# First norm centred and scaled 1024 columns at a time in place, and half of the key weights' subtractions moved to GpSimd

## The chip, the cores and the metric

The kernel runs on one core of one Trainium2 chip. The metric is device time in microseconds (us) of one execution; the median of three runs of the kernel before is 990.82 us. Engines are named as in the profile: PE (TensorE matmuls), PEld (its weight loads), DVE (VectorE), ACT (ScalarE), POOL (GpSimd), SP (the queue that issues most DMAs).

## What is computed

A trunk of two layers over 256 tokens of width 2048: first a Mamba-2 layer, then a layer of sliding-window attention. Each ends in a residual sum and a layer norm. The change lies where the first layer ends and the second begins:

```python
x = _layernorm(ALPHA * x + h, ln_g[0], ln_b[0])    # end of the Mamba-2 layer
...
kv = x @ kv_w + kv_b                               # shared keys and values: 2048 x 512
...
proj = x @ w_in                                    # queries and gates: 2048 x 4096

def _layernorm(x, g, b):
    mu = jnp.mean(xf, axis=-1, keepdims=True)
    var = jnp.mean(jnp.square(xf - mu), axis=-1, keepdims=True)
    return (xf - mu) * lax.rsqrt(var + EPS) * g + b
```

## The kernel before

**Products.** Every float32 product is made of three matmuls in the fp32r type: each operand is split into a high part (a rounded copy) and a low part (the operand minus its high part), and high x high, high x low and low x high are summed in PSUM.

**Weight units.** Weights come from HBM in units of 128 x 2048, each as two halves of 128 x 1024. SP loads a half into a raw buffer `wr` (five of them). ACT copies it into the high part `wh` (`load_unit`, L143), and DVE subtracts: `wl = wr - wh` (L144). `wh` and `wl` have four buffers each, so the copy of a new unit waits until PE has done with the unit four places earlier; a raw buffer is free for the next load when its subtraction has read it. The numbers behind the names count buffers: the four units of the keys' and values' weights (`wkv`) have `wl_881`, `wl_886`, and then `wl_916` and `wl_920` before, `wl_908` and `wl_912` in the changed kernel.

**The end of the first layer.** The 256 tokens are two row halves, h = 0 and h = 1, of 128 tokens; both lie in `xr`. `out_last` multiplies the last group of the Mamba layer with four units of the output weights. For each unit (512 columns, `nb`) PE makes 12 matmuls (L330 to L332), DVE adds the sum to `xr` (L337) and takes statistics (L809). All four column blocks of h = 0 come first, and then `done1(0)` runs; blocks 1 to 3 of h = 1 follow, and then `done1(1)`.

**`done1(h)`**, the first norm, takes mean and variance together (L813), makes the reciprocal deviation on ACT (L815, L816), and then goes through four blocks c of 512 columns: DVE centres and multiplies by the gain (L831, from `xr` into a buffer `t`), scales and adds the bias (L834, back to `xr`); PE transposes the block, four matmuls against the identity (L839, into PSUM); ACT copies the result into the high part `x1H` (L844), DVE makes the low part `x1L` (L845).

**Keys and values.** `x_stat` (L881 to L883) multiplies `x1H` and `x1L` with the four `wkv` units, for h = 0 and then for h = 1: 48 matmuls each. L881 needs `x1H` and `wh`, L882 `x1L`, L883 `wl`. Unit i uses the columns of block c = i of the norm; its first two of four steps read the first halves of `wh` and `wl`, the last two the second halves. Of the bias of keys and values POOL issues the load (L859), and the sums are added on DVE (L897, L901).

**The order.** In the Mamba layer the order on each engine is that of the code. In everything named above a scheduler sets it, engine by engine, by its own costs and priorities; each engine then works through its row strictly in that order.

Of the kernel before, what the change touches and what calls it, by code (L numbers as in the profile page):

```python
# [8 lines left out]
F32 = mybir.dt.float32  # L9
# [3 lines left out]
ALU = mybir.AluOpType  # L13
AX = mybir.AxisListType

P = 128
# [3 lines left out]
NG = 8  # L20
# [42 lines left out]
def trunk(ctx: ExitStack, tc: tile.TileContext, A: dict, out: bass.AP, dbg=None):  # L63
    nc = tc.nc
    PSUM = bass.MemoryType.PSUM

    def pool(name, bufs=1, side=None, space=None, stack=ctx):
        kw = {"space": space} if space is not None else {}
        return stack.enter_context(
            tc.tile_pool(name=name, bufs=bufs, side=side, reuse_waits="tile", **kw)  # L70
        )
# [9 lines left out]
    def nm(s):  # L81
        uid[0] += 1
        return f"{s}_{uid[0]}"
# [4 lines left out]
    def ax_tile():  # L88
        return ax_ps.tile([P, 512], F32, tag="ax", name=nm("ax"), bufs=4)
# [27 lines left out]
    def new_unit(places):  # L117
        u = Unit()
        u.parts = []
        for tag, n, pl in (("wh", NH, places[0]), ("wl", NL, places[1])):  # L120
            t = wp.tile([P, 2112], F32R, tag=tag, name=nm(tag), bufs=n)
            u.parts.append([(t[:, o : o + (k1 - k0) * P], k0, k1) for o, k0, k1 in pl])
        u.h, u.l = u.parts[0][0][0], u.parts[1][0][0]
        return u
# [3 lines left out]
    def load_half():  # L128
        if halves:
            n, c = halves.pop(0)  # L130
            raws[n, c] = raw = wp.tile([P, 1024], F32, tag="wr", name=nm("wr"), bufs=NR)
            nc.sync.dma_start(raw[:], srcs[n][:, c * 1024 : (c + 1) * 1024])

    def load_unit(n, places):
        u = new_unit(places)
        for c in range(2):
            half = raws.pop((n, c))
            for (h, k0, k1), (l, _, _) in zip(*u.parts):
                a, b = max(k0, 8 * c), min(k1, 8 * c + 8)
                if a < b:  # L140
                    sl = slice((a - k0) * P, (b - k0) * P)
                    raw = half[:, (a - 8 * c) * P : (b - 8 * c) * P]
                    nc.scalar.activation(h[:, sl], raw, AF.Copy)  # L143
                    nc.vector.tensor_tensor(l[:, sl], raw, h[:, sl].bitcast(F32), ALU.subtract)  # L144
            load_half()
        return u

# [72 lines left out]
    srcs = []  # L220

    def wo_srcs(name, j):
        return [A[name][j * 4 + i] for i in range(4)]

    for g in range(NG):
# [3 lines left out]
                srcs.append(A["wo"][(g - 1) * 4 + OUT_AT[g].index(b)])  # L229
        if g > 0:  # L230
            srcs += [A["wo"][(g - 1) * 4 + i] for i in range(len(OUT_AT[g]), 4)]
    srcs += wo_srcs("wo", NG - 1) + [A["wkv"][i] for i in range(4)]
    broken = set()
    for what, j in B_ORDER:
        if what == "g":
# [13 lines left out]
    def fill_units():  # L249
        while len(units) < min(used[0] + ahead[0], len(srcs)):  # L250
            n = len(units)
            if n == MORE_AT:
                ahead[0] = AHEAD
            if n in XK_AT:
                i = XK_AT.index(n)
                nc.sync.dma_start(xr[:, i, :], A["xk"][:, i, :])
            if n - 2 in XK_AT:
                i = XK_AT.index(n - 2)
                nc.scalar.activation(xr[:, i, :], xr[:, i, :], AF.Copy, scale=ALPHA)
            units.append(load_unit(n, BROKEN if n in broken else [WHOLE, WHOLE]))  # L260
# [35 lines left out]
    xr = xr_all[:, : 2 * D].rearrange("p (h d) -> p h d", h=2)  # L296
# [44 lines left out]
    def out_last(aH, aL, rms, stats, done):  # L341

        us = []
        for nb in range(4):
            us.append(next_unit())
            out_unit(aH, aL, 0, us[nb], nb, False, rms)
            stats(0, nb)
            if nb == 0:
                out_unit(aH, aL, 1, us[nb], nb, False, rms)
                stats(1, nb)  # L350
        done(0)
        for nb in range(1, 4):
            out_unit(aH, aL, 1, us[nb], nb, False, rms)
            stats(1, nb)
        done(1)
# [403 lines left out]
    for g in range(NG):  # L759
        t = 10 * g  # L760
# [47 lines left out]
    def norm_stats(st, h, nb):  # L808
        nc.vector.bn_stats(st[:, h, nb, :], xr[:, h, nb * 512 : (nb + 1) * 512])  # L809

    def norm_scale(lp, st, h):
        mv = lp.tile([P, 2], F32, tag="mv", name=nm("mv"), bufs=2)
        nc.vector.bn_aggr(mv[:], st[:, h, :, :])  # L813
        rs = lp.tile([P, 1], F32, tag="rs", name=nm("rs"), bufs=2)
        nc.scalar.activation(rs[:], mv[:, 1:2], AF.Ln, bias=eps_t[:])  # L815
        nc.scalar.activation(rs[:], rs[:], AF.Exp, scale=-0.5)  # L816
        return mv, rs

    with ExitStack() as s2:
        lp = pool("lp", stack=s2)  # L820
        gb = lp.tile([P, 2, D], F32, tag="gb", name="gb1")
        nc.gpsimd.dma_start(gb[:, 0, :], A["lng"][0].partition_broadcast(P))
        nc.gpsimd.dma_start(gb[:, 1, :], A["lnb"][0].partition_broadcast(P))
        st1 = lp.tile([P, 2, 4, 6], F32, tag="st", name="st1")

        def done1(h):
            mv, rs = norm_scale(lp, st1, h)
            for c in range(4):
                sl = slice(c * 512, (c + 1) * 512)
                t = lp.tile([P, 512], F32, tag="t", name=nm("t"), bufs=2)  # L830
                nc.vector.scalar_tensor_tensor(  # L831
                    t[:], xr[:, h, sl], mv[:, 0:1], gb[:, 0, sl], ALU.subtract, ALU.mult
                )
                nc.vector.scalar_tensor_tensor(  # L834
                    xr[:, h, sl], t[:], rs[:], gb[:, 1, sl], ALU.mult, ALU.add
                )
                ps = ax_tile()
                for k in range(4):
                    nc.tensor.transpose(  # L839
                        ps[:, k * P : (k + 1) * P], xr[:, h, c * 512 + k * P : c * 512 + (k + 1) * P], ident  # L840
                    )
                dst = (slice(None), slice(c * 4, c * 4 + 4), slice(h * P, (h + 1) * P))
                psv = ps[:].rearrange("p (k t) -> p k t", k=4)
                nc.scalar.activation(x1H[dst], psv, AF.Copy)  # L844
                nc.vector.tensor_tensor(x1L[dst], psv, x1H[dst].bitcast(F32), ALU.subtract)  # L845

        if PRE:
            tc.keep_in_program_order(nc.scalar.preload_act_table_set("natural_log_exp_and_others"))
        out_last(*gs[NG - 1].y, gs[NG - 1].rms, lambda h, nb: norm_stats(st1, h, nb), done1)
    a_stack.close()  # L850

# [393 lines left out]
```

## Time and profile before

| | |
|---|---|
| median of 3 runs (990.53 to 991.11) | 990.82 us |
| profiled execution, its time | 993.6 us |
| its span, first to last instruction | 991.8 us |
| its mean granted TensorE clock | 0.994 |
| PE busy | 980.7 us, 99% of the span |
| DVE busy | 795.7 us, 80% |
| ACT busy | 534.5 us, 54% |
| POOL busy | 170.1 us, 17% |

Times inside the kernel are counted from the span's start. The norm and the keys' and values' products take the stretch from about 650 to 690. "x2" behind a row says that two neighbouring instructions of one form are shown as one row, with the time from the start of the first to the end of the second. In square brackets stands the idle time ahead of an instruction, and what ended it. A row of the form "746/750/1794" gives the shortest, the median and the longest duration in ns. POOL's subtractions, of which the change makes four, have no row in this profile; POOL's other two-input operations have.

### The profile page before, as it was taken

The page shows a single profiled execution, that of the slowest core. Times are in us where ns is not written, and L with a number is a line of the kernel's source. Part 1 is how long each engine was busy: PE and PEld are TensorE (multiplying, and loading weights), DVE is VectorE, ACT ScalarE, POOL GpSimd, SP SyncE. Part 2 cuts the span into 40 slices and gives each one's busy share as a digit, 9 for nine tenths or more (in the row PEclk, how much of TensorE's full clock was granted, in tenths as well). Part 3 has the DMA queues.
Part 4 walks back from the last instruction along what each step waited for, and adds up shares of the span by engine and source line. Part 5 has one row for each costly group of instructions (what it writes and reads, how often), then busy time and mean ns, then how long its engine had stood idle before and what let it go on. Part 6 is the DMA issues. An engine that isn't in the chain of part 4 may idle for free.

```text
span 991.8 us, 17619 instructions
## 1 busy us (share of the span) xinstructions
PE 980.7 (99%) x6868; PEld 881.7 (89%) x6868; DVE 795.7 (80%) x1227; ACT 534.5 (54%) x905; POOL 170.1 (17%) x225
## 2 busy tenths in 40 slices
PE   9999999999999999999999999999999999999997
PEld 7999989999998998999999999877898888878875
DVE  6879887976987887796797697999658687878686
ACT  6586747455644835744745554444446454635432
POOL 0004004005046002200400400500202222221102
PEclk9999999999999999999999999999999999999998
DMA  9588885686585666658558657646774849584932
GB/s 367 178 281 271 253 290 153 187 298 174 172 306 178 209 197 242 203 183 308 151 186 304 170 171 261 241 147 218 226 234 140 313 153 327 166 305 119 340 115 86
DMA packets 69443, 218.72 MB, mean 221 GB/s; under 512 B 8096, under 2 KB 19632, under 8 KB 68592
## 3 DMA queue, kind: packets, MB, share of 16 engines
q1 hardware_dynamic: 63648, 198.95, 61.5%
q0 software_dynamic: 5424, 18.12, 5.4%
q8 instruction: 54, 0.88, 0.4%
q10 hardware_dynamic: 288, 0.52, 0.1%
q14 instruction: 29, 0.24, 0.1%
HBM read 205.37 MB, written 12.19 MB: 219 GB/s over the span
## 4 chain that ended last, share of the span: by engine, by line
PE 78%; DVE 11%; ACT 4%; DMA 4%; issue 3%; POOL 0%; DVEq 0%; SPq 0%; POOLq 0%; ACTq 0%
PE mm L269 14%; PE mm L270 14%; PE mm L271 14%; PE mm L330 7%; PE mm L331 7%; PE mm L332 7%; PE mm L881 3%; DVE wl L144 3%; PE mm L882 3%; PE mm L883 3%; PE ax L609 2%; ACT wh L143 1%; DMA pd<-z 1%; PE ax L1007 1%; DMA gb<-in_lng 1%
## 5 line engine op out<-in xcount | busy, mean ns | idle before, releaser
L144 DVE TENSOR_TENSOR wl<-wr,wh 128x1024 fp32r<-128x1024 f32 (+2 forms) x338 | 398.6, 1209 | 92.7 <-ACT wh L143 91.8
L143 ACT ACTIVATE wh<-wr 128x1024 fp32r<-128x1024 f32 (+2 forms) x338 | 328.9, 1012 | 197.1 <-PE mm L331 71.7
L269 PE MATMUL mm<-xH,wh 128*128 128x256 f32 x1280 | 356.2, 278 | 0.0
L270 PE MATMUL mm<-xL,wh 128*128 128x256 f32 x1280 | 355.2, 278 | 0.0
L271 PE MATMUL mm<-xH,wl 128*128 128x256 f32 x1280 | 354.9, 277 | 0.0
L269 PEld LDWEIGHTS mm<-xH,wh 128*128 128x128 f32 x1280 | 240.8, 188 | 3.5 <-issue 0.9
L270 PEld LDWEIGHTS mm<-xL,wh 128*128 128x128 f32 x1280 | 240.8, 188 | 1.0
L271 PEld LDWEIGHTS mm<-xH,wl 128*128 128x128 f32 x1280 | 240.7, 188 | 0.0
L626 POOL TENSOR_TENSOR yz<-yz,z 128x256 f32<-128x256 f32 x32 | 33.3, 1060 | 437.6 <-DVE yz L620 431.5
L330 PE MATMUL mm<-wh,yH 128*128 128x512 f32 x256 | 101.4, 396 | 1.9 <-DVE xr L337 1.9
L331 PE MATMUL mm<-wh,yL 128*128 128x512 f32 x256 | 100.0, 391 | 0.0
L332 PE MATMUL mm<-wl,yH 128*128 128x512 f32 x256 | 99.8, 390 | 0.0
L457 DVE SCALAR_TENSOR_TENSOR cv<-mm,pc,cv 128x255 f32<-128x255 f32 x144 | 69.2, 481 | 15.3 <-ACT cv L455 11.8
L270 PE MATMUL mm<-x1L,wh 128*128 128x256 f32 x256 | 70.9, 277 | 0.0
L269 PE MATMUL mm<-x1H,wh 128*128 128x256 f32 x256 | 70.8, 277 | 0.0
L271 PE MATMUL mm<-x1H,wl 128*128 128x256 f32 x256 | 70.8, 277 | 0.0
L881 PE MATMUL mm<-wh,x1H 128*128 128x512 f32 x160 | 63.8, 398 | 0.0
L883 PE MATMUL mm<-wl,x1H 128*128 128x512 f32 x160 | 62.8, 392 | 0.3 <-DVE wl L144 0.2
L882 PE MATMUL mm<-wh,x1L 128*128 128x512 f32 x160 | 62.7, 392 | 0.2 <-DVE x1L L845 0.2
L455 ACT ACTIVATE cv<-mm,pc 128x256 f32<-128x256 f32 x48 | 26.8, 558 | 63.6 <-PE mm L271 63.5
L330 PEld LDWEIGHTS mm<-wh,yH 128*128 128x128 f32 x256 | 48.1, 188 | 12.5 <-DVE xr L337 2.3
L332 PEld LDWEIGHTS mm<-wl,yH 128*128 128x128 f32 x256 | 48.1, 188 | 10.1
(222 smaller groups left out, 1378.7 us busy)
## 6 DMA issues: line engine op xcount, KB each, us to landing
wr<-in_wa SPq DMA_DIRECT2D x154, 512.0 KB, 5.3
wr<-in_wo SPq DMA_DIRECT2D x64, 512.0 KB, 5.1
wr<-in_wq SPq DMA_DIRECT2D x32, 512.0 KB, 5.1
wr<-in_wg SPq DMA_DIRECT2D x32, 512.0 KB, 5.4
wr<-in_wb SPq DMA_DIRECT2D x32, 512.0 KB, 5.3
rb<-rscr SPq DMA_DIRECT2D x16, 512.0 KB, 5.9
el<-rscr SPq DMA_DIRECT2D x16, 256.0 KB, 7.6
wr<-in_wkv SPq DMA_DIRECT2D x8, 512.0 KB, 6.6
```

Source lines behind the costliest of these rows:

```text
L143: nc.scalar.activation(h[:, sl], raw, AF.Copy)
L144: nc.vector.tensor_tensor(l[:, sl], raw, h[:, sl].bitcast(F32), ALU.subtract)
L269: nc.tensor.matmul(ps, ah, bh, start=first, stop=False)
L270: nc.tensor.matmul(ps, ah, bl, start=False, stop=False)
L271: nc.tensor.matmul(ps, al, bh, start=False, stop=last)
L330: nc.tensor.matmul(ps[:], aH[:, k, hs], u.h[:, ks], start=k == 0, stop=False)
L331: nc.tensor.matmul(ps[:], aL[:, k, hs], u.h[:, ks], start=False, stop=False)
L332: nc.tensor.matmul(ps[:], aH[:, k, hs], u.l[:, ks], start=False, stop=k == 3)
L457: nc.vector.scalar_tensor_tensor(a[:, sft:], ps[:, : S - sft], w(3 - sft), a[:, sft:], ALU.mult, ALU.add)
L881: nc.tensor.matmul(ps[:], x1H[:, kk, hs], u.h[:, ks], start=kk == 0, stop=False)
L882: nc.tensor.matmul(ps[:], x1L[:, kk, hs], u.h[:, ks], start=False, stop=False)
L883: nc.tensor.matmul(ps[:], x1H[:, kk, hs], u.l[:, ks], start=False, stop=kk == KT - 1)
```

## The change

In `done1` the two DVE operations are done on 1024 columns, at c = 0 and c = 2, and in place: the buffer `t` goes. So eight operations for each row half become four. Transposes and splits stay at 512 columns. In `load_unit` the subtraction of the second half (c = 1) of the four `wkv` units goes to GpSimd.

```diff
-                    nc.vector.tensor_tensor(l[:, sl], raw, h[:, sl].bitcast(F32), ALU.subtract)
+                    eng = nc.gpsimd if c and len_a <= n < len_a + 4 else nc.vector
+                    eng.tensor_tensor(l[:, sl], raw, h[:, sl].bitcast(F32), ALU.subtract)
...
-    srcs += wo_srcs("wo", NG - 1) + [A["wkv"][i] for i in range(4)]
+    srcs += wo_srcs("wo", NG - 1)
+    len_a = len(srcs)
+    srcs += [A["wkv"][i] for i in range(4)]
...
             for c in range(4):
-                sl = slice(c * 512, (c + 1) * 512)
-                t = lp.tile([P, 512], F32, tag="t", name=nm("t"), bufs=2)
-                nc.vector.scalar_tensor_tensor(
-                    t[:], xr[:, h, sl], mv[:, 0:1], gb[:, 0, sl], ALU.subtract, ALU.mult
-                )
-                nc.vector.scalar_tensor_tensor(
-                    xr[:, h, sl], t[:], rs[:], gb[:, 1, sl], ALU.mult, ALU.add
-                )
+                if c % 2 == 0:
+                    v = xr[:, h, c * 512 : (c + 2) * 512]
+                    g, b = [gb[:, i, c * 512 : (c + 2) * 512] for i in range(2)]
+                    nc.vector.scalar_tensor_tensor(v, v, mv[:, 0:1], g, ALU.subtract, ALU.mult)
+                    nc.vector.scalar_tensor_tensor(v, v, rs[:], b, ALU.mult, ALU.add)
```

The diff adds lines, so numbers shift: L144 becomes L145, L330 to L332 become L333 to L335, L337 becomes L340, L809 becomes L812, L813 becomes L816; the two operations of the norm, L831 and L834, become L835 and L836; L839 to L883 stay.

The scheduler also writes another order around the norm. DVE, from the mean and variance of h = 0 on, before:

```order
L813 BN_AGGR mv_890_7586<-st1_7479 128x2
L831 SCALAR_TENSOR_TENSOR t_892_7591<-xr_76,mv_890_7586,gb1_7476 128x512
L831 SCALAR_TENSOR_TENSOR t_894_7601<-xr_76,mv_890_7586,gb1_7476 128x512
L834 SCALAR_TENSOR_TENSOR xr_76<-t_892_7591,rs_891_7588,gb1_7476 128x512
L144 TENSOR_TENSOR wl_886_7562<-wr_868_7420,wh_885_7561 128x1024
L144 TENSOR_TENSOR wl_886_7562<-wr_877_7515,wh_885_7561 128x1024
L845 TENSOR_TENSOR x1L_7472<-ax_893_7594,x1H_7471 128x4x128
L834 SCALAR_TENSOR_TENSOR xr_76<-t_894_7601,rs_891_7588,gb1_7476 128x512
L831 SCALAR_TENSOR_TENSOR t_896_7611<-xr_76,mv_890_7586,gb1_7476 128x512
L831 SCALAR_TENSOR_TENSOR t_898_7621<-xr_76,mv_890_7586,gb1_7476 128x512
```

DVE at the same place in the changed kernel:

```order
L816 BN_AGGR mv_890_7586<-st1_7479 128x2
L835 SCALAR_TENSOR_TENSOR xr_76<-xr_76,mv_890_7586,gb1_7476 128x1024 x2
L145 TENSOR_TENSOR wl_886_7562<-wr_868_7420,wh_885_7561 128x1024
L836 SCALAR_TENSOR_TENSOR xr_76<-xr_76,rs_891_7588,gb1_7476 128x1024 x2
L340 SCALAR_TENSOR_TENSOR xr_76<-mm_896_7623,r_872_7453,xr_76 128x512
L845 TENSOR_TENSOR x1L_7472<-ax_892_7593,x1H_7471 128x4x128
L845 TENSOR_TENSOR x1L_7472<-ax_893_7600,x1H_7471 128x4x128
L845 TENSOR_TENSOR x1L_7472<-ax_894_7609,x1H_7471 128x4x128
L845 TENSOR_TENSOR x1L_7472<-ax_895_7616,x1H_7471 128x4x128
```

All 2048 columns are now centred first, then one weight half is subtracted, then all columns are scaled; before, the first 512 columns were scaled ahead of that weight unit.

PE, with the first transposes of h = 0, before (the block of `xr` that they turn goes to `ax_893`):

```order
L331 MATMUL mm_901_7646<-wh_865_7412,yL_864_7403 128x512
L332 MATMUL mm_901_7646<-wl_866_7413,yH_863_7402 128x512
L839 MATMUL ax_893_7594<-cc_69,xr_76 128x128 x4
L330 MATMUL mm_901_7646<-wh_865_7412,yH_863_7402 128x512
L331 MATMUL mm_901_7646<-wh_865_7412,yL_864_7403 128x512
```

PE with all transposes of h = 0 in the changed kernel; the first row here stands twelve matmuls behind the second row above:

```order
L335 MATMUL mm_898_7653<-wl_876_7512,yH_863_7402 128x512
L839 MATMUL ax_892_7593<-cc_69,xr_76 128x128 x4
L839 MATMUL ax_893_7600<-cc_69,xr_76 128x128 x4
L333 MATMUL mm_898_7653<-wh_875_7511,yH_863_7402 128x512
L839 MATMUL ax_894_7609<-cc_69,xr_76 128x128 x4
L839 MATMUL ax_895_7616<-cc_69,xr_76 128x128 x4
L334 MATMUL mm_898_7653<-wh_875_7511,yL_864_7403 128x512
L335 MATMUL mm_898_7653<-wl_876_7512,yH_863_7402 128x512
L333 MATMUL mm_898_7653<-wh_875_7511,yH_863_7402 128x512
L334 MATMUL mm_898_7653<-wh_875_7511,yL_864_7403 128x512
L335 MATMUL mm_898_7653<-wl_876_7512,yH_863_7402 128x512
L881 MATMUL mm_906_7716<-wh_880_7536,x1H_7471 128x512
```

The sixteen transposes now stand close together, ahead of the first matmul for the keys; before, the last eight stood between the first of those. For h = 1 they likewise move into one place.

POOL in the changed kernel, behind the loads of gain and bias (before, those were followed by the loads of `snk` and `bias` directly):

```order
L826 DMA gb1_7476<-in_lnb 128x2048
L145 TENSOR_TENSOR wl_881_7537<-wr_867_7416,wh_880_7536 128x1024
L145 TENSOR_TENSOR wl_886_7562<-wr_877_7515,wh_885_7561 128x1024
L145 TENSOR_TENSOR wl_908_7718<-wr_882_7540,wh_907_7717 128x1024
L145 TENSOR_TENSOR wl_912_7740<-wr_887_7565,wh_911_7739 128x1024
L855 DMA snk_7710<-in_snk 128x32
L859 DMA bias_905_7714<-in_kvb 128x512
```

The four subtractions now stand ahead of those two loads. On ACT the copies of the third `wkv` unit (`wh_907`) now stand ahead of the four copies into `x1H` of h = 0, and those of the fourth (`wh_911`) behind them. From the sums of h = 1 (L897 for the second time) on every engine has its old order again.

## The prediction

> **What bounds the kernel now.** I read the page's engine shares first, then PE's timeline through the stage of the norm, then DVE's and ACT's beside it, and last every place where POOL and DVE run side by side.
>
> ```profile
> PE 980.7 (99%) x6868; PEld 881.7 (89%) x6868; DVE 795.7 (80%) x1227; ACT 534.5 (54%) x905; POOL 170.1 (17%) x225
> ```
>
> PE is the bound nearly everywhere, so this stage can give only what PE loses in it. PE there:
>
> ```profile
> 656.06 0.39 PE L332 MATMUL mm<-wl,yH 128*128 128x512 f32 x1
> 656.44 0.63 PE L839 MATMUL ax<-cc,xr 128*128 128x128 f32 x4
> 656.82 0.48 PE L330 MATMUL mm<-wh,yH 128*128 128x512 f32 x1
> 657.14 0.40 PE L331 MATMUL mm<-wh,yL 128*128 128x512 f32 x1
> ...
> 664.14 0.40 PE L882 MATMUL mm<-wh,x1L 128*128 128x512 f32 x1
> ...
> 668.26 0.39 PE L882 MATMUL mm<-wh,x1L 128*128 128x512 f32 x1
> 668.83 0.50 PE L883 MATMUL mm<-wl,x1H 128*128 128x512 f32 x1 [0.17 <-DVE wl L144]
> ...
> 673.88 1.29 PE L839 MATMUL ax<-cc,xr 128*128 128x128 f32 x8 [0.29 <-DVE xr L834]
> 675.20 0.50 PE L881 MATMUL mm<-wh,x1H 128*128 128x512 f32 x1
> 675.93 0.50 PE L882 MATMUL mm<-wh,x1L 128*128 128x512 f32 x1 [0.22 <-DVE x1L L845]
> ...
> 681.00 0.48 PE L881 MATMUL mm<-wh,x1H 128*128 128x512 f32 x1
> ```
>
> Undisturbed matmuls follow each other every 0.229 us (664.14 to 668.26, 18 steps). Four transposes take 0.38 (656.44 to 656.82), and the step after them 0.32, 0.09 more than usual. From the L332 at 656.06 to the L881 at 681.00 PE's row holds 82 matmuls and eight groups of four transposes, in seven runs: 82 x 0.229 + 8 x 0.38 + 7 x 0.09 = 22.45 us. It took 24.94, so 2.5 us are lost, to `wl`, to the scaled `xr` and to `x1L`: all late from DVE. The same two instructions stand in the changed row with the same work between them, only that the groups form four runs (22.2 us). So the change is worth 22.2 - 24.94 = -2.75 us, plus what PE then waits.
>
> **Part one: 1024 columns, in place.** DVE and ACT in h = 0:
>
> ```profile
> 653.92 0.26 DVE L813 BATCH_NORM_AGGREGATE mv<-st 128x2 f32<-128x24 f32 x1
> 654.22 1.41 DVE L831 SCALAR_TENSOR_TENSOR t<-xr,mv,gb 128x512 f32<-128x512 f32 x2
> 655.55 0.74 DVE L834 SCALAR_TENSOR_TENSOR xr<-t,rs,gb 128x512 f32<-128x512 f32 x1
> 656.22 2.35 DVE L144 TENSOR_TENSOR wl<-wr,wh 128x1024 fp32r<-128x1024 f32 x2
> ...
> 664.52 1.28 DVE L845 TENSOR_TENSOR x1L<-ax,x1H 128x512 fp32r<-128x512 f32 x2
> 665.71 1.28 DVE L809 BATCH_NORM_STATS2 st<-xr 128x6 f32<-128x512 f32 x2
> 654.90 2.01 ACT L143 ACTIVATE wh<-wr 128x1024 fp32r<-128x1024 f32 x2 [0.15 <-PE mm L331]
> 658.27 2.01 ACT L143 ACTIVATE wh<-wr 128x1024 fp32r<-128x1024 f32 x2 [0.56 <-PE mm L331]
> ```
>
> A 512-wide operation of the norm occupies DVE for 0.66 us (655.55 - 654.22, halved), a 1024-wide subtraction for 1.13 (2.35 less one of 1.22, at 656.22). A 1024-wide operation of the norm has no row; it lies between 1.13 and 2 x 0.66 = 1.32, and I take 1.2. Four for each h in place of eight save 0.5 us of DVE per h. The price is lumpiness: no column is scaled before all are centred. Centring runs from 654.22 to 656.6, one weight half to 657.75, and undisturbed the scaled halves would be ready at 658.95 and 660.15. PE's twelve matmuls ahead of the transposes cover the first: 656.06 + 13 x 0.229 = 659.04. Covered, the lumps cost nothing; without that cover each tenth of a microsecond of lateness is one for PE.
>
> **Part two: four subtractions on POOL.** They take 4 x 1.13 = 4.5 us from DVE. POOL itself is idle here, and its results are early enough: the tightest, the fourth, is done about 671 by the times below and read by PE about 676. What it does to DVE is another matter:
>
> ```profile
> L1143 DVE SCALAR_TENSOR_TENSOR t<-xr,mv,gb x4: 746/750/1794, 974.8 to 976.8; 128x512 f32<-128x512 f32 x4
> L1147 POOL TENSOR_TENSOR xr<-t,gb x4: 1272/1426/1747, 976.5 to 980.9; 128x512 f32<-128x512 f32 x4
> L339 DVE TENSOR_TENSOR xr<-xr,mm x3: 669/674/689, 978.5 to 981.2; 128x512 f32<-128x512 f32 x3
> L144 DVE TENSOR_TENSOR wl<-wr,wh x338: 244/1220/1760, 21.2 to 961.5; 128x1024 fp32r<-128x1024 f32 x153, 128x128 fp32r<-128x128 f32 x8, 128x896 fp32r<-128x896 f32 x8
> L630 POOL TENSOR_TENSOR sq<-yz x32: 608/1191/1610, 90.4 to 632.5; 128x256 f32<-128x256 f32 x32
> 236.67 3.26 DVE L144 TENSOR_TENSOR wl<-wr,wh 128x1024 fp32r<-128x1024 f32 x2
> 237.24 1.60 POOL L630 TENSOR_TENSOR sq<-yz 128x256 f32<-128x256 f32 x1
> 238.92 1.60 POOL L634 TENSOR_TENSOR sq<-sq,sq 128x256 f32<-128x256 f32 x1
> ```
>
> The last norm has the very form of the new one (two tensors from SBUF). Where a 512-wide POOL operation came in between, one DVE operation took 1794 ns in place of 746: it stood for 1.05 us. Subtractions on DVE stand 0.54 us (1760 against 1220) for a 256-wide one, and POOL stands a whole DVE subtraction in turn (1.60 against 0.61). An operation with one input in PSUM (L339) does not stand at all. The two take turns: whoever waits gets in when the other's instruction ends. From 0.54 at 256 and 1.05 at 512 the hold grows 0.51 per 256, so 2.1 us at 1024; the ends are 1.05 (if it is let go halfway) and 4.0 (four of the longer 256-wide durations, near 1 us).
>
> POOL's first subtraction, for `wl_881`, falls between 647 and 650, beside sums and statistics on DVE that do not stand. Now the second, for `wl_886`. ACT's second copy ends at 654.90 + 2.01 = 656.9, and POOL stands behind DVE's weight half until 657.75. Then it goes ahead of L836, the scaling: that runs 659.85 to 661.05, 2.1 late. The third unit's copies on ACT (the row at 658.27) wait for PE's last use of `wh_865`, which without the transposes in between ends about 657.6 (five matmuls behind 656.06, and 0.39 for the last), and take 2.0, so POOL's third subtraction is ready at 659.7, asks when its second is done, about 660.1, and goes in between the two scalings: 661.05 to 663.15. The second scaling ends at 664.35. With 0.1 for the signal:
>
> - first transposes: 661.15 instead of 659.04, PE waits 2.1;
> - eight transposes and a matmul (0.76 + 0.32) end at 662.23; the second half comes at 664.45, PE waits 2.2.
>
> Behind that: DVE's sum of h = 1, four `x1L` and the remaining sums and statistics have one SBUF tensor each and go undisturbed to 670.5 (one L337 0.66, four L845 2.4, and two more L337 and three L809 3.1). POOL's fourth subtraction (ACT's copies wait for PE and end about 668.7) holds until 670.8, so DVE loses 0.3. Two weight halves, the mean and the norm of h = 1 then end at 676.9 and 678.05. PE reaches these transposes at 664.45 + 0.76 + 0.32 + 4 x 0.229 + 46 x 0.229 = 677.0, and the second pair at 678.1: no further wait. Sum: -2.75 + 2.1 + 2.2 = +1.6 us.
>
> The rest costs nothing as long as its cover stands. Gain and bias are read as before. POOL's load of the bias of keys and values now waits behind four subtractions until about 671:
>
> ```profile
> bias<-in_kvb POOLq DMA_DIRECT2D x1, 256.0 KB, 3.6
> ```
>
> It lands about 675 and is wanted at 679; later, it would hold L897 on DVE, with queries' weights behind it that PE wants only near 690. SP's loads wait for raw buffers that POOL lets go up to 2 us later; the first of the queries' units is copied when `wh_880` falls free, near 682, some 5 us after its second half lands. From there on each step is paced by PE, so the delay stays to the end.
>
> **The clock.** PE's two waits come within 5.3 us. What such a wait did elsewhere in this trace (columns: window, then length, PE busy, PEld, DVE, ACT, POOL, granted clock, DMA share, GB/s):
>
> ```profile
> 938.94:942.35 3.41, 1.46 (x6) 0.87 (x6) 3.32 (x4) 0.76 (x1) 0.00 (x0) 1.00 0.91 376
> 942.35:945.76 3.41, 3.41 (x9) 2.65 (x8) 3.41 (x6) 0.00 (x0) 0.00 (x0) 0.50 0.84 256
> ...
> 123.16:126.57 3.41, 1.97 (x9) 1.31 (x7) 3.41 (x4) 1.33 (x2) 0.00 (x0) 1.00 1.03 368
> 126.57:129.98 3.41, 2.99 (x14) 2.50 (x15) 3.41 (x5) 1.06 (x1) 0.00 (x0) 1.00 0.87 276
> ```
>
> With 1.46 us of work in 3.41, the next 3.41 us ran at clock 0.50; with 1.97, they did not. Our two waits leave about 1.3 us of work in the 3.41 us around them, wherever the grid of windows falls, so a slow window is near certain. It costs half of PE's work in it: nothing where it covers the second wait, 1.7 us behind it, up to 2.5 if two follow. Over the positions of the grid I get 1.2 on average. +1.6 + 1.2 = +2.8 us.
>
> Two pages of the Trainium skill bear on this. SBUF — State Buffer, § Who interferes with whom, says that the port pair shared by VectorE and GpSimd is held for the full instruction; the rows at 256 and 512 agree, and no row here shows 1024. TensorE: Matmul & The Clock Gate, § Why this matters for your kernels, puts the drop at PE-idle gaps above some 3 us; by that rule neither wait is long enough and the sum stays at +1.6, but the row at 938.94, with 1.95 us without a matmul, speaks against it.
>
> **Baseline.** The profiled execution took 993.6 us (span 991.8 and 1.8 around it), 2.8 above the median of 990.82. I add the difference to the median: 990.8 + 2.8 = 993.6.
>
> **Rivals.** 0.2%, 2.0 us, is about what a measurement of this kernel can tell from no change.
>
> 1. *The clock holds:* waits as above, no slow window: +1.6, 992.4. For it: the window at 126.57. Against: 938.94. Chance 0.13.
> 2. *POOL gets in once, or lets go halfway:* one wait of 2.2, or two of about 1.1. -2.75 + 2.25 = -0.5, 990.3. For it: no row as wide as 1024. Against: POOL's third is ready 1.3 us before DVE's first scaling ends, and the turns at 236 to 240 are strict. Chance 0.18.
> 3. *The other side: DVE keeps its turn.* At 657.75 POOL has asked for 0.85 us, but the two scalings stand back to back in DVE's queue. If they go through first, they end at 658.95 and 660.15, PE waits for neither, and POOL runs beside L340 and L845, which do not stand: all of the 2.75 is won, 988.1. It is decided at 657.75 alone. For it: every turn in the trace is of a 256- or 512-wide POOL operation. Against: between two norm operations of the last norm POOL did get in (the 1794 ns). Chance 0.14.
> 4. *POOL is slower than the line through 256 and 512:* the fp32r output on POOL has no row. With a hold of 4.0, 2 x 1.9 = 3.8 more than +1.6, with a slow window: 997. Chance 0.12.
>
> The forecast itself has 0.43.
>
> **Numbers.** Likeliest 993.6, its own range 992.0 to 995.2 (hold 1.9 to 2.3, slow window 0 to 2.5). The range for 8 in 10 takes in rivals 1 and 2 and parts of 3 and 4: 989.0 to 996.2. Slower by over 0.2% (above 992.8): 0.8 of the forecast, a quarter of rival 1, all of rival 4: 0.34 + 0.03 + 0.12 = 0.49. Faster (below 988.8): nearly all of rival 3, 0.13. Within: 0.38.
>
> **What would show it.** Right: L836 rows of about 3.3 us in place of 1.3, POOL's L145 at 2.3 us alone and 3.4 behind DVE, two PE waits near 2 us for `xr` at L839, a window of clock 0.50 after them. Wrong: L836 at 1.3 us, L839 without a wait, and the stretch from 656 to 681 shorter by more than 2 us. POOL rows above 4 us speak for rival 4. The prediction fails as a whole if the queries' stage after 690 wins or loses time of its own.

## The result, and the profile after

The changed kernel takes 992.95 us (median of 11 runs, 991.37 to 995.30); the kernel before, in 11 runs, 990.28 us (988.78 to 991.95). The ratio is 1.0033, with a 95% interval of 1.0024 to 1.0041: slower by 2.4 to 4.1 us. The profiled execution of the changed kernel took 992.95 us as well (span 991.1).

The engine shares of its page, to be set against those of before:

```profile
PE 978.8 (99%) x6868; PEld 882.3 (89%) x6868; DVE 796.6 (80%) x1215; ACT 534.4 (54%) x905; POOL 181.3 (18%) x229
```

VectorE has twelve instructions less and yet is busy 0.9 us longer. Its timeline through the norm of h = 0, and that of GpSimd beside it:

```profile
654.07 0.26 DVE L816 BATCH_NORM_AGGREGATE mv<-st 128x2 f32<-128x24 f32 x1
654.37 2.48 DVE L835 SCALAR_TENSOR_TENSOR xr<-xr,mv,gb 128x1024 f32<-128x1024 f32 x2
656.77 1.22 DVE L145 TENSOR_TENSOR wl<-wr,wh 128x1024 fp32r<-128x1024 f32 x1
657.91 6.70 DVE L836 SCALAR_TENSOR_TENSOR xr<-xr,rs,gb 128x1024 f32<-128x1024 f32 x2
...
671.07 2.93 DVE L145 TENSOR_TENSOR wl<-wr,wh 128x1024 fp32r<-128x1024 f32 x1
...
677.57 2.47 DVE L836 SCALAR_TENSOR_TENSOR xr<-xr,rs,gb 128x1024 f32<-128x1024 f32 x2
648.45 2.39 POOL L145 TENSOR_TENSOR wl<-wr,wh 128x1024 fp32r<-128x1024 f32 x1 [13.30 <-ACT wh L143]
657.14 6.39 POOL L145 TENSOR_TENSOR wl<-wr,wh 128x1024 fp32r<-128x1024 f32 x2 [6.30 <-ACT wh L143]
670.53 2.40 POOL L145 TENSOR_TENSOR wl<-wr,wh 128x1024 fp32r<-128x1024 f32 x1 [7.00 <-ACT wh L143]
```

The two scalings of h = 0 take 6.70 us, those of h = 1 take 2.47. Their groups over both h (count; shortest, median and longest in ns; first and last start):

```profile
L836 DVE SCALAR_TENSOR_TENSOR xr<-xr,rs,gb x4: 1272/2324/3406, 657.9 to 678.8; 128x1024 f32<-128x1024 f32 x4
L835 DVE SCALAR_TENSOR_TENSOR xr<-xr,mv,gb x4: 1264/1274/1285, 654.4 to 676.4; 128x1024 f32<-128x1024 f32 x4
L145 POOL TENSOR_TENSOR wl<-wr,wh x4: 2389/2741/3334, 648.5 to 670.5; 128x1024 fp32r<-128x1024 f32 x4
```

GpSimd's subtraction takes 2389 ns alone, and a scaling that it gets ahead of stands 3406 - 1272 = 2134 ns. PE, its waits and the matmuls around them; the first and the last row are the two instructions between which the prediction counts PE's work (L332 at 656.06 and L881 at 681.00 before):

```profile
656.21 0.39 PE L335 MATMUL mm<-wl,yH 128*128 128x512 f32 x1
...
658.93 0.39 PE L335 MATMUL mm<-wl,yH 128*128 128x512 f32 x1
661.46 1.06 PE L839 MATMUL ax<-cc,xr 128*128 128x128 f32 x8 [2.14 <-DVE xr L836]
662.28 0.56 PE L333 MATMUL mm<-wh,yH 128*128 128x512 f32 x1
664.76 1.94 PE L839 MATMUL ax<-cc,xr 128*128 128x128 f32 x8 [1.91 <-DVE xr L836]
666.35 0.78 PE L334 MATMUL mm<-wh,yL 128*128 128x512 f32 x1
...
679.42 1.03 PE L839 MATMUL ax<-cc,xr 128*128 128x128 f32 x8
...
685.05 0.39 PE L881 MATMUL mm<-wh,x1H 128*128 128x512 f32 x1
```

The stretch in windows of 3.41 us (columns as in the prediction):

```profile
659.11:662.52 3.41, 1.27 (x10) 1.01 (x9) 3.41 (x2) 1.06 (x2) 3.41 (x2) 1.00 0.76 210
662.52:665.93 3.41, 1.50 (x8) 1.20 (x7) 3.41 (x4) 0.74 (x3) 1.01 (x1) 0.50 0.56 172
665.93:669.34 3.41, 3.41 (x11) 2.83 (x10) 3.20 (x6) 2.04 (x3) 0.00 (x0) 0.50 0.18 73
669.34:672.75 3.41, 3.41 (x16) 2.81 (x16) 3.41 (x4) 1.11 (x2) 2.22 (x1) 1.00 0.01 2
```

PE stands twice, 2.14 and 1.91 us; each wait leaves 1.3 to 1.5 us of work in its window, and the window behind it runs at clock 0.50. The 1.50 + 3.41 us of busy time at half clock are 2.5 us of work lost. In h = 1 the profile shows no wait of PE.

To compare kernels I use one length, called the stage below: from VectorE's mean of h = 0 to PE's first 256-wide matmul of the queries. In before it runs from the L813 at 653.92 (in the prediction) to the first of these two rows, in after from the L816 at 654.07 to the second:

```profile
711.27 0.28 PE L269 MATMUL mm<-x1H,wh 128*128 128x256 f32 x1
```

```profile
715.23 0.28 PE L272 MATMUL mm<-x1H,wh 128*128 128x256 f32 x1
```

That is 57.35 us before and 61.16 after: +3.81. The profiled span of before is nevertheless the longer one (991.8 against 991.1), as behind the stage it has 280.5 us where the trace of after and those of the twelve experiments have 275.1 to 276.9: the wait of 1.95 us and the slow window at 938.94 to 945.76, which the prediction quotes, belong to that one execution.

### The profile page after: what moved, and what is told of

Its sections match the earlier page's. It is cut to its first block, busy times and chain, and to the rows that moved or that the text cites. A ratio compares the mean times of both kernels' runs of the same rounds, so it can differ in the third digit from the quotient of the medians.

```text
span 991.1 us, 17615 instructions
## 1 busy us (share of the span) xinstructions
PE 978.8 (99%) x6868; PEld 882.3 (89%) x6868; DVE 796.6 (80%) x1215; ACT 534.4 (54%) x905; POOL 181.3 (18%) x229
## 4 chain that ended last, share of the span: by engine, by line
PE 87%; DVE 7%; ACT 3%; issue 1%; DMA 1%; SPq 0%; DVEq 0%; ACTq 0%
PE mm L272 15%; PE mm L273 15%; PE mm L274 15%; PE mm L333 8%; PE mm L334 8%; PE mm L335 8%; PE mm L881 4%; PE mm L882 4%; PE mm L883 4%; DVE wl L145 2%; PE ax L612 2%; PE ax L1065 1%; DMA rb<-rscr 1%; PE ax L1007 1%; ACT wh L143 1%
## 5 line engine op out<-in xcount | busy, mean ns | idle before, releaser
L145 DVE TENSOR_TENSOR wl<-wr,wh 128x1024 fp32r<-128x1024 f32 (+2 forms) x334 | 395.0, 1212 | 92.1 <-ACT wh L143 91.0
L333 PE MATMUL mm<-wh,yH 128*128 128x512 f32 x256 | 101.6, 397 | 1.9 <-DVE xr L340 1.9
L335 PE MATMUL mm<-wl,yH 128*128 128x512 f32 x256 | 100.2, 391 | 0.0
L881 PE MATMUL mm<-wh,x1H 128*128 128x512 f32 x160 | 63.6, 398 | 0.0
L883 PE MATMUL mm<-wl,x1H 128*128 128x512 f32 x160 | 62.4, 390 | 0.0
L333 PEld LDWEIGHTS mm<-wh,yH 128*128 128x128 f32 x256 | 48.2, 188 | 12.7 <-DVE xr L340 2.3
L335 PEld LDWEIGHTS mm<-wl,yH 128*128 128x128 f32 x256 | 48.3, 189 | 10.2
```

The source lines that it names most:

```text
L145: eng.tensor_tensor(l[:, sl], raw, h[:, sl].bitcast(F32), ALU.subtract)
L333: nc.tensor.matmul(ps[:], aH[:, k, hs], u.h[:, ks], start=k == 0, stop=False)
L335: nc.tensor.matmul(ps[:], aH[:, k, hs], u.l[:, ks], start=False, stop=k == 3)
L881: nc.tensor.matmul(ps[:], x1H[:, kk, hs], u.h[:, ks], start=kk == 0, stop=False)
L883: nc.tensor.matmul(ps[:], x1H[:, kk, hs], u.l[:, ks], start=False, stop=kk == KT - 1)
```

## Experiments

Theory A: GpSimd's hold on VectorE makes the scaled `xr` late, PE waits, and the clock drops behind the waits. Theory B: it is the lumps of 1024 columns, or the order of VectorE's work, whoever subtracts. All times are medians of 7 to 12 runs beside runs of the kernel before on the same chip. One table for all:

| kernel | us | ratio to before, 95% interval | stage, us | PE's waits in it, us |
|---|---|---|---|---|
| before | 989.5 to 990.3 | | 57.35 | 0.3, 0.2, 0.2 |
| after | 992.95 | 1.0033 (1.0024, 1.0041) | 61.16 | 2.1, 1.9 |
| 1 wide norm alone | 992.01 | 1.0024 (1.0014, 1.0035) | 59.54 | 1.9, 0.3 |
| 2 GpSimd alone | 992.08 | 1.0023 (1.0013, 1.0033) | 59.43 | 2.1, 1.8 |
| 3 wide, GpSimd for the first unit | 991.31 | 1.0017 (1.0007, 1.0027) | 57.91 | 1.9, 0.3 |
| 4 after, pieces of 256 | 988.71 | 0.9993 (0.9984, 1.0001) | 56.04 | 0.5, 0.4 |
| 5 after, pieces of 512 | 990.28 | 1.0004 (0.9992, 1.0015) | 57.15 | 1.1, 0.9 |
| 6 after, pieces of 128 | 990.39 | 1.0008 (1.0000, 1.0017) | 59.00 | 0.2, 2.0 |
| 7 in place, 512 wide | 989.07 | 0.9994 (0.9985, 1.0002) | 57.33 | 0.3, 0.2, 0.2 |
| 8 in place 512, pieces of 256 | 990.08 | 1.0001 (0.9992, 1.0011) | 57.46 | 0.5, 1.2, 0.3 |
| 9 wide in h = 0 alone | 988.83 | 0.9990 (0.9981, 1.0000) | 56.90 | 0.3, 0.2 |
| 10 pieces of 256 and 128 | 989.59 | 0.9997 (0.9985, 1.0008) | 57.23 | 0.2, 1.5 |
| 11 as 4, again | 988.45 | 0.9991 (0.9982, 1.0001) | 56.03 | 0.5, 0.4 |
| 12 pieces, three units | 987.41 | 0.9982 (0.9971, 0.9994) | 55.76 | 0.2, 0.3 |

The stage comes from one execution each, the time from all; the clock alone can make them differ by up to 2.5 us, what it took in after. A second difference lies outside the profiled span. In 4, 5, 8 and 11 every run's time is 2.1 to 2.4 us above its span; in the other kernels it is 1.7 to 1.9, but for one run of 6 (2.3). Why stays open. By the medians of the spans, 4 is 1.7 us and 11 is 1.6 us shorter than before, so the times of these four kernels show some 0.5 us less of a gain than the spans do.

**1. The wide norm alone.** From after:

```diff
-eng = nc.gpsimd if c and len_a <= n < len_a + 4 else nc.vector
+eng = nc.vector
```

> Part one alone: the norm 1024 columns at a time in place, all weight subtractions on VectorE. Theory A (GpSimd's hold is what costs): every L836 row near 1.27 us; both weight halves (2.3 us) now stand ahead of the scalings, so the first scaling ends near 660.3 and PE waits about 1.1 us for it once and hardly at all for the second; no window at half clock, or one. Stage 656 to 681 about 1.5 us shorter than before, 988.8 us (988 to 990.3). Theory B (the lumps of 1024 columns cost by themselves, wherever the subtractions are): two waits for xr near 2 us and half clock behind them, 992 to 993.

It took 992.01 us, 2.1 more than before, and theory A's 988.8 is missed. In h = 0 nothing holds VectorE: the scalings take 1.24 us each. The wait of 1.1 us expected for PE there did not come. But h = 1 brings a wait that I had not looked for (VectorE's and PE's timelines):

```profile
668.24 1.20 DVE L145 TENSOR_TENSOR wl<-wr,wh 128x1024 fp32r<-128x1024 f32 x1
669.37 0.25 DVE L816 BATCH_NORM_AGGREGATE mv<-st 128x2 f32<-128x24 f32 x1
669.54 1.16 DVE L145 TENSOR_TENSOR wl<-wr,wh 128x1024 fp32r<-128x1024 f32 x1
670.62 2.47 DVE L835 SCALAR_TENSOR_TENSOR xr<-xr,mv,gb 128x1024 f32<-128x1024 f32 x2
673.01 2.47 DVE L836 SCALAR_TENSOR_TENSOR xr<-xr,rs,gb 128x1024 f32<-128x1024 f32 x2
674.43 1.06 PE L839 MATMUL ax<-cc,xr 128*128 128x128 f32 x8 [1.87 <-DVE xr L836]
```

The windows there:

```profile
672.21:675.62 3.41, 1.41 (x10) 0.86 (x8) 3.41 (x4) 0.53 (x2) 0.00 (x0) 1.00 0.51 183
675.62:679.03 3.41, 3.29 (x12) 2.92 (x13) 3.02 (x5) 1.75 (x4) 0.00 (x0) 0.52 0.40 88
```

Two weight halves, two centrings and a scaling stand ahead of the first scaled columns, and half clock follows PE's wait. Here the edit does more than name another engine, as the scheduler has written another row for PE too. Against after, the first transposes of h = 0 stand five matmuls later, which covers the 1.1 us; and those of h = 1 stand behind 38 of the keys' matmuls in place of 46. Eight matmuls are 8 x 0.229 = 1.8 us, about the wait. So theory B has a share, with a condition: where PE asks that early, the lumps cost, in h = 1. Experiment 9 tests it with the same 38.

**2. GpSimd alone.** The four lines of the norm as in before, the subtractions as in after.

```diff
-v = xr[:, h, c * 512 : (c + 2) * 512]
...
+nc.vector.scalar_tensor_tensor(t[:], xr[:, h, sl], mv[:, 0:1], gb[:, 0, sl], ALU.subtract, ALU.mult)
+nc.vector.scalar_tensor_tensor(xr[:, h, sl], t[:], rs[:], gb[:, 1, sl], ALU.mult, ALU.add)
```

> Part two alone: the norm 512 columns at a time through t as before, the four subtractions on GpSimd. Theory A: single 512-wide norm rows of 2.8 us (0.7 + 2.1) in place of 0.75; PE's second to fourth groups of transposes 0.3 to 1.5 us later, as VectorE also has 2.3 us less to do ahead of them; 990.5 to 993. Theory B (the lumps cost): GpSimd takes 4.5 us off VectorE and nothing is lost, 987.5 to 989.

992.08 us, as theory A has it; B's 987.5 to 989 is out. (PE's and VectorE's rows are again not those of either kernel.) Two rows of VectorE's timeline:

```profile
656.89 2.86 DVE L837 SCALAR_TENSOR_TENSOR xr<-t,rs,gb 128x512 f32<-128x512 f32 x1
662.19 3.57 DVE L837 SCALAR_TENSOR_TENSOR xr<-t,rs,gb 128x512 f32<-128x512 f32 x2
```

A 512-wide scaling takes 2.86 us in place of 0.74: the hold of 2.1 us does not depend on the width of what it holds. The two waits of PE are there, 2.12 and 1.76 us, longer than the 0.3 to 1.5 expected.

**3. The wide norm, and GpSimd for one unit.** The first unit's subtraction runs early, beside sums and statistics:

```diff
-eng = nc.gpsimd if c and len_a <= n < len_a + 4 else nc.vector
+eng = nc.gpsimd if c and n == len_a else nc.vector
```

> The wide norm, and GpSimd for the first of the four units alone, whose subtraction runs near 648.5 to 651, beside sums and statistics of VectorE. Theory A: that subtraction holds nothing (L340 and L812 at 0.75 and 0.70 us), every L836 near 1.27 us; PE waits once, about 1.1 us; as wide_only within 0.5 us: 988.7 (988 to 990.3). Theory A is wrong in its part on operations with one SBUF tensor if rows of 2.8 us show near 649. Theory B: as after, 992 to 993.

Missed as the first was, and for the same reason: 991.31 us, with PE's row of the first experiment and the same wait in h = 1. What it adds: beside GpSimd's row VectorE's operations with one tensor in SBUF do not stand (timelines; until 648.7 GpSimd itself stands behind a weight half of VectorE).

```profile
647.57 3.46 POOL L145 TENSOR_TENSOR wl<-wr,wh 128x1024 fp32r<-128x1024 f32 x1 [11.11 <-ACT wh L143]
648.70 0.74 DVE L340 SCALAR_TENSOR_TENSOR xr<-mm,r,xr 128x512 f32<-128x512 f32 x1
649.47 0.69 DVE L812 BATCH_NORM_STATS2 st<-xr 128x6 f32<-128x512 f32 x1
```

And it shows the clock's share apart. Its wait in h = 1 is that of the first experiment (1.91 against 1.87 us), but no slow window follows in the profiled execution (windows laid around the wait):

```profile
671.90:675.31 3.41, 1.50 (x8) 0.96 (x7) 3.41 (x4) 0.00 (x0) 0.00 (x0) 1.00 0.77 276
675.31:678.72 3.41, 3.16 (x22) 2.68 (x21) 3.41 (x5) 2.17 (x4) 0.00 (x0) 1.00 0.20 23
```

The stage is 57.91 us here and 59.54 there: 1.6 us for one window.

**4, 5, 6. After, with GpSimd's subtractions in pieces.** The rows of VectorE, ACT and PE are those of after, instruction by instruction; only the length of one GpSimd instruction changes. (`w` is the width of a piece; the condition around the loop is left out here.)

```diff
-eng.tensor_tensor(l[:, sl], raw, h[:, sl].bitcast(F32), ALU.subtract)
+for i in range(1024 // w):
+    q = slice(i * w, (i + 1) * w)
+    nc.gpsimd.tensor_tensor(l[:, sl][:, q], raw[:, q], h[:, sl][:, q].bitcast(F32), ALU.subtract)
```

With pieces of 256:

> As after, but each of the four subtractions on GpSimd is written as four of 256 columns. VectorE's work and its order are those of after. Theory A (the hold lasts as long as GpSimd's instruction, and the two engines take turns): each L836 row 1.27 + 0.54 = 1.8 us in place of 3.4, PE waits 0.6 and 0.5 us in place of 2.1 and 1.9, no window at half clock; 988.7 (988 to 990.3), faster than before. Theory C (VectorE stands until GpSimd has nothing left in its queue, or the loss comes from the order of VectorE's work): L836 rows stay near 3.4 us and the time near 993. GpSimd's four pieces together take 2.4 to 3 us.

With 512:

> As after, with each of GpSimd's subtractions in two pieces of 512 columns; VectorE's order is that of after and of the pieces of 256. If the hold follows the width (0.48 us at 256, 2.13 at 1024): 1.05 us, the two L836 in h = 0 near 2.3 us each, PE waits 1.0 and 0.9 us for xr, the stage 1.0 us longer than with pieces of 256: 989.8 us, up to 1 us more if a window at half clock follows the waits. If the loss at 1024 were a matter of one wide instruction alone, and any cut does away with it: 988.7, as with 256.

With 128:

> As after, with each of GpSimd's subtractions in eight pieces of 128 columns. If the hold follows the width: 0.25 us, L836 near 1.5 us, PE waits 0.2 and 0.1 us, the stage 0.5 us shorter than with pieces of 256: 988.2 us. Against it: each instruction of GpSimd brings a fixed part of its own, so that eight may take 4 us and more, and the third and fourth subtraction come too late for PE (a wait for wl at L883): 989 to 991.

The two scalings of h = 0 (groups of VectorE within the stretch; count, then busy time and mean ns), in after and with pieces of 512, 256 and 128:

```profile
L836 DVE SCALAR_TENSOR_TENSOR xr<-xr,rs,gb 128x1024 f32<-128x1024 f32 x2 | 6.7, 3390 | 0.0
```

```profile
L840 DVE SCALAR_TENSOR_TENSOR xr<-xr,rs,gb 128x1024 f32<-128x1024 f32 x2 | 4.5, 2304 | 0.0
```

```profile
L840 DVE SCALAR_TENSOR_TENSOR xr<-xr,rs,gb 128x1024 f32<-128x1024 f32 x2 | 3.4, 1754 | 0.0
```

```profile
L840 DVE SCALAR_TENSOR_TENSOR xr<-xr,rs,gb 128x1024 f32<-128x1024 f32 x2 | 2.9, 1482 | 0.0
```

Less the 1272 ns of an undisturbed one, the hold is 2.12, 1.03, 0.48 and 0.21 us. It is halved with the width, and PE's waits follow it (2.1 and 1.9; 1.1 and 0.9; 0.5 and 0.4; 0.2). With 256 the time is the 988.7 expected, though its interval still holds 1, so "faster than before" is not shown by it. With 512 it is 990.28, inside the 989.8 to 990.8 expected. That settles theory A for h = 0, and theory C, that VectorE stands until GpSimd has nothing left, is out there.

But 128 took 990.39 us and not 988.2. VectorE's weight half of the third unit, in h = 1, stood (VectorE, GpSimd and PE there):

```profile
666.51 4.12 DVE L149 TENSOR_TENSOR wl<-wr,wh 128x1024 fp32r<-128x1024 f32 x1
667.84 1.71 POOL L147 TENSOR_TENSOR wl<-wr,wh 128x128 fp32r<-128x128 f32 x4
670.68 0.50 PE L887 MATMUL mm<-wl,x1H 128*128 128x512 f32 x1 [2.00 <-DVE wl L149]
```

GpSimd's pieces follow one another here without a gap until 669.5, and the weight half ends 1.1 us later, the time that it needs: at some seven ends of a piece in a row GpSimd went first again, while VectorE's half had begun. The late wait that I had named against 128 came, but from VectorE's half, not from GpSimd's. Behind it the clock drops in this execution: over the stage it is 0.97 on average, against 1.00 with the other widths of piece.

**7. In place, 512 wide, all on VectorE.**

```diff
-v = xr[:, h, c * 512 : (c + 2) * 512]
+v = xr[:, h, c * 512 : (c + 1) * 512]
```

> In place, but 512 columns at a time, all subtractions on VectorE: the norm's order and lumps are those of before, only t is gone. If wide_only loses by its width (all centring ahead of all scaling, and two weight halves ahead of the norm of h = 1): this is as before, 989.9 (989 to 990.8), with no wait of PE over 0.5 us for xr. If it loses by working in place: 991.5 to 992.5.

(The line that names the engine is that of 1.) As before: 989.07 us, a ratio of 0.9994 whose interval holds 1, PE's row instruction by instruction that of before, and the stage within 0.02 us. In place costs nothing. What is left is the width, with the order that the scheduler makes of it.

**8. The same with pieces of 256 on GpSimd.** The norm of 7 and the pieces of 4 together, of which this is the second part:

```diff
-eng.tensor_tensor(l[:, sl], raw, h[:, sl].bitcast(F32), ALU.subtract)
+for i in range(4):
+    q = slice(i * 256, (i + 1) * 256)
+    nc.gpsimd.tensor_tensor(l[:, sl][:, q], raw[:, q], h[:, sl][:, q].bitcast(F32), ALU.subtract)
```

> In place 512 columns at a time, and GpSimd's four subtractions in pieces of 256. VectorE has five norm operations beside GpSimd's pieces in place of two; each may stand 0.48 us. PE's transposes are asked for later, one group at a time. Near the wide norm with pieces: 988.7 (988 to 990); below 988.4 if the finer groups save PE both of its waits, above 989.3 if five holds (2.4 us) reach it.

990.08 us, in the case named for holds that reach PE, and a little past the range. Its VectorE rows show them: two centrings 2.47 us in place of 1.41, two scalings 2.45, and PE waits 1.19 us for the third group. Narrow norm operations meet more pieces.

**9. Wide in h = 0, 512 in h = 1, all on VectorE.**

```diff
+w = 1024 if h == 0 else 512
+if c * 512 % w == 0:
+    v = xr[:, h, c * 512 : c * 512 + w]
```

> The wide norm for h = 0 alone, 512 columns in place for h = 1, all subtractions on VectorE. In wide_only PE waited 1.9 us once, in h = 1, where two weight halves stand ahead of four wide operations on VectorE, and half clock followed. If that is all that part one costs: the scaled first half of h = 1 is ready 0.9 us earlier (two centrings and two scalings of 512 in place of two centrings and one scaling of 1024: 2.8 against 3.7 us), PE waits 0.9 us or less, and the time is 989 to 990, as before. If the wide form costs in h = 0 as well: 991 to 992.

(The engine again as in 1.) 988.83 us, with a wait of 0.27 in h = 1. PE asks behind 38 of the keys' matmuls as in 1, so the wait of 1.87 there is the width's. The loss of the wide norm alone lies in h = 1, where VectorE has two weight halves ahead of it; in h = 0 the lumps are covered.

**10 and 11. What kept VectorE out?** The second and third unit in pieces of 128, the first and fourth in pieces of 256; beside it the kernel of 4 once more.

```diff
-for i in range(4):
-    q = slice(i * 256, (i + 1) * 256)
+w = 128 if n in (len_a + 1, len_a + 2) else 256
+for i in range(1024 // w):
+    q = slice(i * w, (i + 1) * w)
```

> As after, GpSimd's subtractions in pieces: 128 columns for the second and third unit, which run beside the scalings of h = 0, 256 for the first and fourth. With 128 throughout, VectorE's weight half near 666.5 stood 3.0 us while eight pieces of the fourth unit ran back to back. If it is pieces that short which don't let VectorE in: here the fourth unit's are 256 wide, that row takes 1.2 to 1.9 us, the L836 rows 1.5 us, and the time is 988.2. If it is rather that GpSimd, once it is ahead, keeps its turn, whatever the width: the row stays near 4 us and the time near 990.4.

> The pieces of 256 once more, beside the mixed ones: L836 rows 1.75 us, PE waits under 0.6 us, 988.7 us (988.2 to 989.3); the interval of its ratio to the kernel before lies below 1.

The mixed kernel took 989.59 us, between the two times named, but its row of 3.58 us decides for the second case. The fourth unit's pieces were 256 wide, and VectorE still stood until GpSimd's last one, which ended near 669.1 (timelines of VectorE and GpSimd; the last four of the twenty are the 256-wide ones):

```profile
666.63 3.58 DVE L150 TENSOR_TENSOR wl<-wr,wh 128x1024 fp32r<-128x1024 f32 x1
656.89 12.23 POOL L148 TENSOR_TENSOR wl<-wr,wh 128x128 fp32r<-128x128 f32 x20 [5.79 <-ACT wh L143]
```

So it is not pieces of 128 that stand in the way. The twenty pieces form one run without a wait, and VectorE asks in the first of the fourth unit's pieces, as it did with 128. With 256 throughout, these start afresh after a wait for ACT (0.18 us), VectorE asks in the third of them and gets in at its end (the repeated kernel):

```profile
667.24 3.82 POOL L147 TENSOR_TENSOR wl<-wr,wh 128x256 fp32r<-128x256 f32 x4 [0.18 <-ACT wh L143]
669.05 1.41 DVE L149 TENSOR_TENSOR wl<-wr,wh 128x1024 fp32r<-128x1024 f32 x1
```

The repeated kernel took 988.45 us; its interval ends at 1.0001, so by its time it is not shown to be faster than before, as had been expected.

**12. Nothing left on GpSimd when VectorE asks.** As the mixed kernel, with the fourth unit's half back on VectorE:

```diff
-if c and len_a <= n < len_a + 4:
+if c and len_a <= n < len_a + 3:
```

> As the mixed pieces (first unit in pieces of 256, second and third of 128), but the fourth unit's subtraction stays on VectorE, so GpSimd has nothing left when VectorE comes to its weight half near 666.5. If that half stood because GpSimd kept the port through an unbroken run of pieces: it takes 1.2 us again, PE waits for no wl, only 0.2 us for xr, and the stage is 0.7 us shorter than with pieces of 256: 988.0 us (987.5 to 988.8), faster than before. If something else made it late (its load, its buffer): it stays near 3.6 us and the time near 989.6. A new wait of up to 1 us may show in h = 1, where VectorE has one subtraction more.

987.41 us, 0.9982 (0.9971 to 0.9994): faster than both kernels, and just below the range expected. The stage is 0.3 us shorter than with pieces of 256 (11), where 0.7 had been expected; about half of the 1.0 us between the two times lies outside the span. The weight half is back at 1.2 us, and PE has two short waits, 0.22 for `xr` and 0.25 for `x1H`. The rows to set against those of 10:

```profile
657.63 9.44 POOL L148 TENSOR_TENSOR wl<-wr,wh 128x128 fp32r<-128x128 f32 x16 [6.63 <-ACT wh L143]
667.36 1.21 DVE L150 TENSOR_TENSOR wl<-wr,wh 128x1024 fp32r<-128x1024 f32 x1
```

## Why the prediction was right, point by point

- **The stage's own loss, -2.75 us.** Borne out: in after, PE's work from the L335 at 656.21 to the L881 at 685.05 took 28.84 us. Less the two waits (4.05) and the 2.5 lost to the clock that is 22.3, where 22.2 was forecast. The best kernel has a stage of 55.76 us, 1.6 shorter than before, with 0.5 us of waits left in it.
- **The 1024-wide operation, 1.2 us.** Measured 2.48 - 1.27 = 1.21. In place is free (7).
- **"Covered, the lumps cost nothing."** True of h = 0 (1, 9). For h = 1 the forecast counted on 51 matmuls of PE between the last transposes of h = 0 and those of h = 1, 46 of them for the keys; after has these 51, and no wait. With 38 the wide norm alone costs a wait of 1.9 us (1). That is why the two parts do not add up. Alone each loses 2.1 or 2.2 us; together they lose 2.4 to 4.1, as in after the holds of h = 0 are there, but PE asks for h = 1 eight matmuls later. It is not that GpSimd's help makes VectorE earlier in h = 1: counted from the mean of h = 0, the first half of h = 1 is scaled after 19.6 us in 1 and after 20.0 in 4.
- **The hold, 2.1 us, bounds 1.05 to 4.0.** Measured 2.13; the line through 0.54 and 1.05 held up to 1024 columns. The fp32r output adds nothing that shows: 2.39 us alone, where 2.3 was expected, so rival 4 falls.
- **The turns.** As forecast: GpSimd went ahead of both scalings, 2.14 and 1.91 us of PE's waiting for 2.1 and 2.2. Rival 2 (one turn, or half a hold) and rival 3 (VectorE keeps its turn) fall with the 6.70 us row. The Trainium skill (SBUF — State Buffer, § Who interferes with whom) says that the shared pair is held for the whole instruction; the four widths agree, but for some 0.25 us of each (below).
- **The clock, 1.2 us on average of 0 to 2.5.** The profiled execution lost 2.5, the upper end. Runs can differ by this term: experiment 2 has the same two waits, no slow window in its trace, and that execution, at 989.79 us, is the fastest of its twelve, 2.3 below their median. By the rule of the Trainium skill (TensorE: Matmul & The Clock Gate, § Why this matters for your kernels) neither wait was long enough for a drop; the row at 662.52, behind a gap of 2.14 us, differs, and the measurement decides. Rival 1 (the clock holds) is what the traces of 2 and 3 show behind such waits; of after there is one trace, and its window was slow.
- **The sum.** For the profiled execution -2.75 + 2.14 + 1.91 + 2.5 = +3.8, against +3.81 in the stage and 28.84 - 24.94 = +3.90 between the two instructions. The medians differ by 2.7 where +2.8 was forecast. That they agree so closely is luck in part: the clock's term could have been anything from 0 to 2.5.
- **The fourth subtraction, 0.3 us.** Mis-sized: ACT's copy came later behind PE's waits, GpSimd began at 670.53, and VectorE's half took 2.93 us in place of 1.2. It cost nothing, as the step said, because PE was later still, by 0.6 us: the first half was scaled at 678.84, and there is no wait at 679.42.
- **The baseline.** Adding the difference to the median was right. The 2.8 us by which the profiled execution of before lay above it came from the wait and the slow window near 940: the stretch behind the stage is at least 3.6 us shorter in each of the other traces.

## What to carry to other kernels

Before a step goes to an idle GpSimd, look at what VectorE does beside it: operations with two tensors in SBUF stood for nearly all of GpSimd's instruction (2.13 of 2.39 us), operations with one did not (0.74 and 0.69 us beside it). Cut GpSimd's instruction until its hold is smaller than the slack of what VectorE makes next, and see that it does not run on without a gap into the next thing that VectorE needs. Width saves VectorE's fixed parts (1.21 us for 1024 columns against twice 0.67) and makes results later, so a wide operation belongs where a cover stands in front of the consumer, and it must be looked for at each place where the code runs, not at the first alone, and anew in each kernel that the scheduler writes: in 1 it had moved eight matmuls.

## What had not been expected of the hardware

- **VectorE can be shut out for longer than one instruction.** Between scalings and pieces the two engines took strict turns (rows of 1.48 us, one hold of 0.21 each). In the runs of 24 and 20 pieces without a gap VectorE's weight half asked with seven and three pieces still to come and got in only behind the last: 4.12 and 3.58 us for 1.2. With the run of pieces gone it took 1.21. By the rule of the Trainium skill (SBUF — State Buffer, § Who interferes with whom: whoever issues first has the pair for its whole instruction, and the other blocks) there would be one hold there, 0.21 or 0.48 us by the widths above; these two rows differ from it. Why the turns are kept at one place and not at the other stays open. The runs show that the fourth unit's pieces make it (12), and that it came where these followed on without a gap and VectorE asked in their first (6, 10), not where they began afresh and it asked in their third (4, 11). Which of the two counts is not shown.
- **The hold is a little shorter than the instruction.** A piece of 128, 256, 512 or 1024 columns takes 0.45, 0.73, 1.29 or 2.39 us on average beside sums and statistics (the first unit's, from experiments 6, 11, 5 and after; the row of 1024 stands above) and holds VectorE for 0.21, 0.48, 1.03 or 2.13. Some 0.25 us of each do not hold. The three groups:

```profile
L147 POOL TENSOR_TENSOR wl<-wr,wh 128x128 fp32r<-128x128 f32 x8 | 3.4, 453 | 12.6 <-ACT wh L143 12.6
```

```profile
L147 POOL TENSOR_TENSOR wl<-wr,wh 128x256 fp32r<-128x256 f32 x4 | 2.8, 732 | 12.2 <-ACT wh L143 12.2
```

```profile
L147 POOL TENSOR_TENSOR wl<-wr,wh 128x512 fp32r<-128x512 f32 x2 | 2.5, 1292 | 12.3 <-ACT wh L143 12.3
```

- **A wait under 2 us is enough for half clock, but not each time.** Behind a wait of 1.87 us in one execution the clock was 0.52 for a window of 3.41 us; behind one of 1.91 at the same place in another it stayed at 1.00.
